# Later modulation vectors and residual additions on VectorE alone, with their loads spread differently over the stages of a decoder layer

## The chip, the cores and the metric

The kernel runs on one core of one Trainium2 chip. The metric is the device time of one execution in microseconds (us); lower is better. All arithmetic is in float32, and the large products are made from float32 numbers split into a high and a low part.

## The reference

One decoder layer: an adaLN-conditioned mixer (sparse attention and stick-breaking attention on eight heads each), then an adaLN-conditioned mixture of 32 experts. What the change touches are the six modulation vectors and the gated residual:

```
mod = jax.nn.silu(c) @ w_mod[l] + b_mod[l]                    # (1, 2048) @ (2048, 6 * 2048)
sh1, sc1, g1, sh2, sc2, g2 = split(mod, 6)
h = rms_norm(x, ln1_g[l]) * (1.0 + sc1) + sh1
x = x + g1 * hybrid_mixer(h, w_in[l], ..., w_out[l])          # 512 tokens, 2048 wide
h = rms_norm(x, ln2_g[l]) * (1.0 + sc2) + sh2
x = x + g2 * hierarchical_moe(h, router_g, router_e, w_gate[l], w_up[l], w_down[l])
```

Each expert has three matrices of 4 MB, so the 32 experts are 403 MB of weights, all of which are read.

## The kernel before

The program has two halves. In the first it makes h, the projections (stages named B0 to B5 and Q0 to Q3, each a 2048 x 512 or 512 x 512 piece of a weight), the two attentions, and the output projection (stages O0 to O5: O0 and O1 are the first two weight tiles of output columns 0 to 511 and 512 to 1023, O2 and O3 the other two, O4 and O5 all four of the third and fourth column block). In the second half it works through 16 pairs of experts.

Every engine runs its own instructions in the order in which the program writes them. All weights go through one list, `items`, which the SyncE queue loads in order into 8 KB slots of one pool of 23 (`big`); a load waits until its slot is free. A weight tile of 1 MB is used in two halves: ScalarE copies the high part into a tile `hl`, VectorE (GpSimd in Q0 to B3) subtracts it to get the low part, and TensorE makes 24 matmuls of 128x512 from it. The halves are prepared one half ahead of their use (two in B0).

The four later modulation vectors (SC2, G1, SH2, G2, in this order) are made row block by row block: 16 loads of 1 MB each (`w_m`, 128 x 2048), and for each one `acc += w * s` with a scalar for each partition (`gemv`). Before, VectorE takes the first 1280, 1536, 1280 or 768 columns of SC2, G1, SH2 and G2; for the rest ScalarE multiplies and GpSimd adds. `MODS` says how many of the 61 loads (three come earlier) go between the weight tiles of each group of stages in `SEGS`: B0 B4 Q2 Q3, then Q0 Q1 B1, then B3, B5, O0 O1, and O2 to O5. Each `gemv` stands on VectorE's queue ahead of the next half's subtraction.

At the end of an output stage `add_up` multiplies the four PSUM tiles by G1 on VectorE and adds them to x; before, GpSimd makes the addition except for the last stage (O5). Beside all this, lanes of attention work (index scores, top-k, softmax, the stick-breaking chains `st`) are stepped between the matmuls; B0 to Q3 and B5 to O0 carry the `st` chains, Q0 to B3 the index, top-k and sparse attention.

Of the kernel before, what the change touches and what calls it, by code (L numbers as in the profile page):

```python
# [15 lines left out]
AF = mybir.ActivationFunctionType  # L16
OP = mybir.AluOpType
# [21 lines left out]

ORDER = ("B0", "B4", "Q2", "Q3", "Q0", "Q1", "B1", "B3", "B5")  # L40
SEGS = ("B0 B4 Q2 Q3", "Q0 Q1 B1", "B3", "B5", "O0 O1", "O2 O3 O4 O5")
MODS = (5, 7, 4, 11, 4, 30)
RATES = (1.2, 1.4, 1.1, 1.5, 0.6, 0.95, 0.2, 0.8, 0.65)
ROOM = (3, 3, 4)
PRE = 3
FAR = ("B0",)
SHARE = 6
CUT = (1280, 1280, 1536, 768)


class Lanes:
# [26 lines left out]
def tile_hybrid_layer(ctx: ExitStack, tc, A, out, dbg=None):  # L78
# [10 lines left out]
    def slot(shape, dt=F32, name="b"):  # L89
        t = big.tile(shape, dt, name=name, tag="b")  # L90
        return t

    def bank(tag, name, dt=F32):
        t = ps.tile([P, 512], dt, name=name, tag=tag)
        return t

    V, G, T, SC, Q = nc.vector, nc.gpsimd, nc.tensor, nc.scalar, nc.sync

    def act(o, i, f=AF.Copy, **kw):
        return SC.activation(o, i, f, **kw)  # L100

    def mm(o, l, r, start, stop, skip=False):
        return T.matmul(o, l, r, start=start, stop=stop, skip_group_check=skip)  # L103
# [5 lines left out]
    def k2(shape, name, dt=F32):  # L109
        t = sm.tile(shape, dt, name=name, tag="k2", bufs=4)  # L110
        return t
# [33 lines left out]
    sil = sm.tile([P, 16], F32, name="sil")  # L145
# [23 lines left out]
    w_dc_v = w_down.rearrange("e (j p) d -> e p j d", p=P)  # L169

    SH1, SC1, G1, SH2, SC2, G2 = range(6)
    CUTS = {SC2: CUT[0], SH2: CUT[1], G1: CUT[2], G2: CUT[3]}
    BCOL = 848

    def src(it):
# [45 lines left out]
    def spread(ws, n):  # L221
        ws = [p for w in ws for p in halves(w)]
        for k, w in enumerate(ws):
            items.append(w)
            for _ in range(n * (k + 1) // len(ws) - n * k // len(ws)):
                items.append(later.pop(0))
# [4 lines left out]
    seg = [sum((work[n] for n in names.split()), []) for names in SEGS]  # L231
    for ws, n in zip(seg, MODS):
        spread(ws, n)
# [36 lines left out]
    accs, rowv = {}, {}  # L270


    def gemv(acc, w, s, cut, first):

        lo, hi = slice(0, cut), slice(cut, acc.shape[-1])
        if first:
            V.tensor_scalar(acc[:, lo], w[:, lo], s, None, op0=OP.mult)
            act(acc[:, hi], w[:, hi], AF.Identity, scale=s)
        else:
            V.scalar_tensor_tensor(acc[:, lo], w[:, lo], s, acc[:, lo], op0=OP.mult, op1=OP.add)  # L280
            act(w[:, hi], w[:, hi], AF.Identity, scale=s)
            G.tensor_tensor(acc[:, hi], acc[:, hi], w[:, hi], op=OP.add)  # L282

    def mod_chunk(v, c, q, lag):

        w = raw.pop(("m", v, c, q))
        if c is None:
            if q == 0:
                accs[v] = slot([P, D], name=f"accv{v}")
                if v in (G1, G2):  # L290
                    G.memset(accs[v], 0.0)
                    G.dma_start(accs[v][0:1], A["b_gate"][int(v == G2):int(v == G2) + 1])
            gemv(accs[v], w, sil[:, q:q + 1], CUTS[v], q == 0 and v not in (G1, G2))
            if q == 15:
                for b in range(4):
                    deferred.append([lag + b // 2, lambda b=b: mod_done(v, b, accs[v][:, 512 * b:512 * b + 512])])
            return
        o, n, r = PIECES[c]
        if q == 0:
            accs[v, c] = k2([P, n], f"acc{v}{c}") if v == SH1 and c else bank("at", f"md{v}{c}")  # L300
        acc = accs[v, c]
        for i in range(r):
            s = sil[:, r * q + i:r * q + i + 1]
            if v == SC1 or c == 0:
                k = 32 * (i % 4)
                mm(acc[k:k + 32, :n], s.to_broadcast([P, 32]), w[:, i], q == 0 and i < 4, r * q + i >= 12, True)
            else:
                gemv(acc, w[:, i], s, n * SHARE // 16, q == 0 and i == 0)

    def first_cols(c):  # L310
        o, n, _ = PIECES[c]
# [31 lines left out]
    def mod_done(v, c, acc):  # L343
        pb = bank("at", f"md{v}{c}")
        if v in (G1, G2):
            mm(pb, ones, acc, True, True)
            act(acc, pb)
            rowv[v] = accs[v]
            return
        l = acc.rearrange("p (q j) -> p j q", j=4)  # L350
        for j in range(4):
            for q in range(4):
                qs = slice(32 * q, 32 * q + 32)
                mm(pb[qs, j:j + 1], l[:, j, qs], one1, True, True)
        cs = slice(4 * c, 4 * c + 4)
        bo, dst = {SC2: (V_SC2, a2), SH2: (V_SH2, sh2)}[v]
        V.tensor_tensor(dst[:, cs], pb[:, :4], vecs[:, bo + 4 * c:bo + 4 * c + 4], op=OP.add)
        if v == SC2:
            V.scalar_tensor_tensor(dst[:, cs], dst[:, cs], 1.0, vecs[:, V_LN2 + 4 * c:V_LN2 + 4 * c + 4],
                                   op0=OP.add, op1=OP.mult)  # L360
# [591 lines left out]
    x1 = []  # L952
# [24 lines left out]
    def main_o(c, q, h, start, stop):  # L977
        wH, wL = HL.pop(("O", c, q, h))
        if start:
            mbanks["b"] = [bank("mm", f"O{c}{i}") for i in range(4)]  # L980
        if q == 0 and h == 0:
            xc = slot([P, 4, 512], name=f"x1_{c}")
            Q.dma_start(xc, x_v[:, :, 512 * c:512 * c + 512])
            x1.append(xc)
        pm = mbanks["b"]
        oH, oL = oS[q // 2, q % 2]
        for t in range(4):
            ts = slice(128 * t, 128 * t + 128)
            for jj in range(2):
                j = 2 * h + jj  # L990
                first, last = start and jj == 0, stop and jj == 1
                mm(pm[t], oH[:, j, ts], wH[:, jj], first, False)
                mm(pm[t], oH[:, j, ts], wL[:, jj], False, False)
                mm(pm[t], oL[:, j, ts], wH[:, jj], False, last)
            if (c, q, h) == (3, 3, 1):
                add_up(c, t, pm, V)
                keep(c, t)
                if t:
                    turn(c, t - 1)
                if t > 1:  # L1000
                    route(c, t - 2)
            yield
        if stop:
            if c == 3:
                turn(c, 3)
                route(c, 2)
                route(c, 3)
                V.tensor_reduce(rs, ssx, axis=AX.X, op=OP.add)
                rstd(r2, rs, D)
            while len(deferred) > (2 if c == 3 else 0):  # L1010
                later_run()
            if c < 3:
                for t in range(4):
                    add_up(c, t, pm, G)
                if q == 3:
                    keep(c)
                    lanes.add(0, resid(c))
# [1 line left out]
    r2, rs = (sm.tile([P, 4], F32, name=n) for n in ("r2", "rs"))  # L1019
    x1T = {}  # L1020

    def add_up(c, t, pm, eng):
        tmp = sm.tile([P, S], F32, name="mix", tag="tmp", bufs=3)
        V.tensor_tensor(tmp, pm[t], rowv[G1][:, 512 * c:512 * c + 512], op=OP.mult)
        eng.tensor_tensor(x1[c][:, t], x1[c][:, t], tmp, op=OP.add)

    x1d = dram.tile([S, D], F32, name="x1d")

    def keep(c, t=None):

        ts = slice(0, 4) if t is None else slice(t, t + 1)
        G.dma_start(x1d.rearrange("(t p) d -> p t d", p=P)[:, ts, 512 * c:512 * c + 512], x1[c][:, ts])

    def turn(c, t):

        pt = bank("at", "x1t")
        for j in range(4):
            T.transpose(pt[:, 128 * j:128 * j + 128], x1[c][:, t].rearrange("p (k j) -> p j k", j=4)[:, j], ident)
        x1T[t] = sm.tile([P, S], F32, name="x1T", tag="rb", bufs=2)
        jk = sm.tile([P, S], F32, name="jk", tag="tmp", bufs=3)  # L1040
        if (c, t) == (3, 3):
            act(jk, x1[c][:, t], AF.Square, accum_out=ssx[:, t, c:c + 1])
            act(x1T[t], pt)
        else:
            act(x1T[t], pt)
            act(jk, x1[c][:, t], AF.Square, accum_out=ssx[:, t, c:c + 1])

    def route(c, t):
        for j in range(4):
            mm(rt[0][:, 36 * t:36 * t + 36], x1T[t][:, 128 * j:128 * j + 128], R3[:, 4 * c + j],  # L1050
               c == 0 and t == 0 and j == 0, c == 3 and t == 3 and j == 3, True)
# [35 lines left out]
    def st(shape, name):  # L1087
# [4 lines left out]
                    op=OP.mult)  # L1092
# [38 lines left out]
    tmp = sm.tile([P, 4, 4, 8], F32, name="lsel", tag="tmp", bufs=3)  # L1131
# [140 lines left out]
    acc = x1  # L1272
# [88 lines left out]
    for n in range(NP):  # L1361
        pgu = []
        i = 24 * n
# [70 lines left out]
    with tc.If(reg > 0):  # L1434
# [13 lines left out]
        with tc.For_i(0, reg, 1):  # L1448
# [23 lines left out]
            for pk, wv in zip(pgu, (w_g_v, w_u_v)):  # L1472
                for c in range(4):
                    w = slot([P, 4, 512], name="wo")
# [5 lines left out]
            for f in range(4):  # L1480
                w = slot([P, D], name="wo")
# [74 lines left out]
```

## Time and profile before

| | |
|---|---|
| median of 3 runs | 1900.78 us (1898.29 to 1902.36) |
| the profiled execution's own time | 1895.36 us |
| its span in the profile | 1893.6 us |
| busy: TensorE, VectorE, ScalarE, GpSimd | 92%, 51%, 32%, 21% of the span |
| data moved | 585.09 MB |

The span is what the profile's times run over; the execution's own time is 1.8 us longer. The shares are means over stages with different limits, so they say little about one stage.

### The profile page before, as it was taken

The numbers are of one execution on the slowest core, as the hardware profiler recorded it, in microseconds if no ns is written. First come the engines' busy times: TensorE is split into PE (matmuls) and PEld (weight loads), VectorE is DVE, ScalarE is ACT, GpSimd is POOL, SyncE is SP. The second block draws the span as 40 slices with busy tenths as digits, with TensorE's granted clock in tenths as the row PEclk, the third lists the DMA queues.
The fourth block names the chain that finished last, engine by engine and source line by source line (L and its number), as shares of the span: only waits on it lengthen the run. The fifth ranks groups of instructions, "written<-read, shape, count | busy, mean of one in ns | idle before, by whom it ended". The sixth has DMA issues, their size and how long they took to land.

```text
span 1893.6 us, 21355 instructions
## 1 busy us (share of the span) xinstructions
PE 1740.0 (92%) x8097; PEld 976.8 (52%) x8097; DVE 973.5 (51%) x1486; ACT 601.5 (32%) x1136; POOL 396.2 (21%) x311
## 2 busy tenths in 40 slices
PE   4999999998999998899899999999999999999997
PEld 1777777765677676787334333333333333333333
DVE  6888722488855668768334334342433243333325
ACT  3645444554556543443222110111012111211010
POOL 3534311333437326656100000000000000000000
PEclk9999999999999998999999999999999999999999
DMA  9878322323226657768899999999999999999997
GB/s 349 285 263 300 123 79 94 133 90 111 90 89 224 227 178 267 267 245 354 359 418 420 419 420 418 420 419 419 419 420 419 420 419 420 419 420 419 419 413 275
DMA packets 136634, 585.09 MB, mean 309 GB/s; under 512 B 10866, under 2 KB 43802, under 8 KB 79270
## 3 DMA queue, kind: packets, MB, share of 16 engines
q1 hardware_dynamic: 132240, 569.09, 76.6%
q0 software_dynamic: 4288, 14.60, 2.1%
q8 instruction: 65, 1.06, 0.2%
q14 instruction: 41, 0.34, 0.0%
HBM read 583.64 MB, written 8.40 MB: 313 GB/s over the span
## 4 chain that ended last, share of the span: by engine, by line
DMA 39%; PE 20%; DVE 6%; issue 4%; ACT 2%; POOL 1%; SPq 0%; DVEq 0%; POOLq 0%; ACTq 0%
DMA w_u<-in_w_up 15%; DMA w_g<-in_w_gate 12%; DMA w_d<-in_w_down 12%; PE O L103 5%; PE y L103 3%; PE u L103 3%; PE g L103 2%; PE B L103 2%; DVE hl L394 1%; PE cb L103 1%; DVE accv L280 1%; DVE x L1288 1%; PE z L103 1%; PE ga L1252 1%; DMA xg<-x1d,gi 1%
## 5 line engine op out<-in xcount | busy, mean ns | idle before, releaser
L103 PE MATMUL u<-w_u,xe 128*64 128x512 f32 x1024 | 265.8, 605 | 24.4 <-DMA w_u<-in_w_up 23.7
L103 PE MATMUL g<-w_g,xe 128*64 128x512 f32 x1024 | 240.9, 596 | 18.4 <-DMA w_g<-in_w_gate 17.4
L1288 DVE TENSOR_TENSOR x<-cb,x 128x512 f32<-128x512 f32 x256 | 157.3, 682 | 186.7 <-PE cb L103 186.7
L103 PE MATMUL y<-w_d,uT 128*64 128x512 f32 x1024 | 236.9, 600 | 0.7 <-ACT uT L100 0.7
L282 POOL TENSOR_TENSOR accv<-accv,w_m_None 128x768 f32<-128x768 f32 (+2 forms) x62 | 153.0, 2468 | 210.6 <-ACT w_m_None L100 124.0
L1230 POOL DMA_INDIRECT xg<-x1d,gi x15 | 15.2, 1016 | 816.4 <-DVE t L1233 654.9
L103 PEld LDWEIGHTS u<-w_u,xe 128*64 128x64 f32 x1024 | 78.2, 138 | 201.5 <-issue 138.1
L103 PEld LDWEIGHTS g<-w_g,xe 128*64 128x64 f32 x1024 | 76.3, 137 | 170.5 <-issue 129.3
L1278 DVE SCALAR_TENSOR_TENSOR yt<-y,gs,accv 128x512 f32<-128x512 f32 x64 | 47.8, 747 | 200.5 <-PE y L103 200.5
L280 DVE SCALAR_TENSOR_TENSOR accv<-w_m_None,sil,accv 128x1280 f32<-128x1280 f32 (+2 forms) x62 | 132.6, 2138 | 6.2 <-issue 5.5
L100 ACT ACTIVATE xe<-ga,modc 128x128 f32<-128x128 f32 x254 | 94.1, 463 | 128.6 <-PE y L103 88.4
L103 PEld LDWEIGHTS y<-w_d,uT 128*64 128x64 f32 x1024 | 66.6, 136 | 116.1 <-issue 106.7
L100 ACT ACTIVATE uT<-uT 128x512 f32<-128x512 f32 x16 | 9.6, 600 | 343.4 <-PE uT L1329 343.4
L103 PE MATMUL cb<-yH,oT 128*128 128x512 f32 x256 | 107.8, 421 | 0.9 <-DVE x L1288 0.9
L100 ACT ACTIVATE yH<-yt 128x512 fp32r<-128x512 f32 x64 | 40.3, 630 | 204.5 <-DVE yt L1278 121.4
L103 PE MATMUL cb<-yL,oT 128*128 128x512 f32 x256 | 101.1, 395 | 0.0
L1280 DVE TENSOR_TENSOR yL<-yt,yH 128x512 fp32r<-128x512 f32 x64 | 44.3, 693 | 110.3 <-PE g L103 63.2
L394 DVE TENSOR_TENSOR hl<-w_O,hl 128x1024 fp32r<-128x1024 f32 x32 | 67.8, 2123 | 40.1 <-ACT hl L100 31.2
L282 POOL TENSOR_TENSOR acc<-acc,w_m 128x160 f32<-128x160 f32 x105 | 61.3, 584 | 70.1 <-ACT w_m L100 62.4
L103 PEld LDWEIGHTS cb<-yH,oT 128*128 128x128 f32 x256 | 48.0, 188 | 49.6 <-issue 38.6
L1252 PEld LDWEIGHTS ga<-cst,xg 128*128 128x128 f32 x252 | 35.2, 209 | 61.8 <-issue 41.0
L1323 DVE TENSOR_TENSOR u<-sg,u 128x512 f32<-128x512 f32 x16 | 11.0, 689 | 105.4 <-PE u L103 105.4
(435 smaller groups left out, 3171.5 us busy)
## 6 DMA issues: line engine op xcount, KB each, us to landing
w_g<-in_w_gate SPq DMA_DIRECT2D x128, 1024.0 KB, 19.9
w_u<-in_w_up SPq DMA_DIRECT2D x128, 1024.0 KB, 21.2
w_d<-in_w_down SPq DMA_DIRECT2D x128, 1024.0 KB, 19.9
w_m_None<-in_w_mod SPq DMA_DIRECT2D x64, 1024.0 KB, 5.0
w_m<-in_w_mod SPq DMA_DIRECT2D x32, 1024.0 KB, 11.0
w_B<-in_w_in SPq DMA_DIRECT2D x48, 512.0 KB, 4.7
w_O<-in_w_out SPq DMA_DIRECT2D x16, 1024.0 KB, 5.9
w_A<-in_w_in SPq DMA_DIRECT2D x8, 848.0 KB, 11.7
```

Of the source, the lines that this page charges most:

```text
L100: return SC.activation(o, i, f, **kw)
L103: return T.matmul(o, l, r, start=start, stop=stop, skip_group_check=skip)
L280: V.scalar_tensor_tensor(acc[:, lo], w[:, lo], s, acc[:, lo], op0=OP.mult, op1=OP.add)
L282: G.tensor_tensor(acc[:, hi], acc[:, hi], w[:, hi], op=OP.add)
L394: low_eng[0].tensor_tensor(t[:, 1], s, t[:, 0].bitcast(F32), op=OP.subtract)
L1230: G.indirect_dma_start(xs, None, x1d[:, :], bass.IndirectOffsetOnAxis(ap=gi[:, 0:1], axis=0), bounds_check=S - 1, oob_is_err=False)
L1252: T.transpose(pb[:, 128 * j:128 * j + 128], xs[:, 512 * c:512 * c + 512].rearrange("p (k j) -> p j k", j=4)[:, j], ident)
L1278: V.scalar_tensor_tensor(yt, y, g, rowv[G2][:, cs], op0=OP.mult, op1=OP.mult)
L1280: V.tensor_tensor(yL[:, cs], yt, yH[:, cs].bitcast(F32), op=OP.subtract)
L1288: return lambda: V.tensor_tensor(acc[q][:, t], pb, acc[q][:, t], op=OP.add)
L1323: V.tensor_tensor(u, sg, pb, op=OP.mult)
```

## The change

Each `gemv` of the four later vectors is one VectorE instruction over all 2048 columns; ScalarE and GpSimd have no part in it any more. The residual additions of all output stages go from GpSimd to VectorE. The loads are dealt out anew by `MODS`. The early vectors (`w_m` in pieces) keep their split, which is now handed in as a number.

```diff
-MODS = (5, 7, 4, 11, 4, 30)
+MODS = (20, 2, 6, 12, 4, 17)
...
-CUT = (1280, 1280, 1536, 768)
...
-    def gemv(acc, w, s, cut, first):
+    def gemv(acc, w, s, first, cut=None):
 
         lo, hi = slice(0, cut), slice(cut, acc.shape[-1])
         if first:
             V.tensor_scalar(acc[:, lo], w[:, lo], s, None, op0=OP.mult)
-            act(acc[:, hi], w[:, hi], AF.Identity, scale=s)
         else:
             V.scalar_tensor_tensor(acc[:, lo], w[:, lo], s, acc[:, lo], op0=OP.mult, op1=OP.add)
-            act(w[:, hi], w[:, hi], AF.Identity, scale=s)
-            G.tensor_tensor(acc[:, hi], acc[:, hi], w[:, hi], op=OP.add)
+        if cut:
+            act(acc[:, hi] if first else w[:, hi], w[:, hi], AF.Identity, scale=s)
+            if not first:
+                G.tensor_tensor(acc[:, hi], acc[:, hi], w[:, hi], op=OP.add)
...
-            gemv(accs[v], w, sil[:, q:q + 1], CUTS[v], q == 0 and v not in (G1, G2))
+            gemv(accs[v], w, sil[:, q:q + 1], q == 0 and v not in (G1, G2))
...
             if c < 3:
                 for t in range(4):
-                    add_up(c, t, pm, G)
+                    add_up(c, t, pm)
...
-        eng.tensor_tensor(x1[c][:, t], x1[c][:, t], tmp, op=OP.add)
+        V.tensor_tensor(x1[c][:, t], x1[c][:, t], tmp, op=OP.add)
```

On VectorE in stage O5 (the last output stage; `accv5` is G2, `hl` the low part of an output weight) these rows stand before:

```order
L394 TENSOR_TENSOR hl_6101<-w_O_3_1_5949,hl_6101 128x1024
L280 SCALAR_TENSOR_TENSOR accv5_5692<-w_m_5_None_9_6048,sil_84,accv5_5692 128x768
L280 SCALAR_TENSOR_TENSOR accv5_5692<-w_m_5_None_10_6094,sil_84,accv5_5692 128x768
L394 TENSOR_TENSOR hl_6138<-w_O_3_2_6099,hl_6138 128x1024
L280 SCALAR_TENSOR_TENSOR accv5_5692<-w_m_5_None_11_6128,sil_84,accv5_5692 128x768
L394 TENSOR_TENSOR hl_6172<-w_O_3_2_6099,hl_6172 128x1024
L280 SCALAR_TENSOR_TENSOR accv5_5692<-w_m_5_None_12_6136,sil_84,accv5_5692 128x768
L394 TENSOR_TENSOR hl_6204<-w_O_3_3_6165,hl_6204 128x1024
```

and these in the changed kernel, at the same place:

```order
L393 TENSOR_TENSOR hl_5996<-w_O_3_1_5813,hl_5996 128x1024
L277 SCALAR_TENSOR_TENSOR accv5_5205<-w_m_5_None_12_5947,sil_84,accv5_5205 128x2048
L393 TENSOR_TENSOR hl_6028<-w_O_3_2_5993,hl_6028 128x1024
L393 TENSOR_TENSOR hl_6057<-w_O_3_2_5993,hl_6057 128x1024
L277 SCALAR_TENSOR_TENSOR accv5_5205<-w_m_5_None_13_6023,sil_84,accv5_5205 128x2048
L393 TENSOR_TENSOR hl_6087<-w_O_3_3_6026,hl_6087 128x1024
```

Fewer modulation steps stand between the subtractions, each over the full width; GpSimd, which had one addition of 1280 columns for each of them, has none.

On VectorE in stage B4 (`accv4` is SC2, `st` the stick-breaking chains) these rows stand before:

```order
L394 TENSOR_TENSOR hl_2053<-w_B_4_0_1961,hl_2053 128x1024
L813 SCALAR_TENSOR_TENSOR st_2095<-z_2096,st_2095 128x384
L813 SCALAR_TENSOR_TENSOR st_2101<-z_2102,st_2101 128x384
L394 TENSOR_TENSOR hl_2147<-w_B_4_1_2018,hl_2147 128x1024
L813 SCALAR_TENSOR_TENSOR st_2095<-z_2157,st_2095 128x384
L813 SCALAR_TENSOR_TENSOR st_2101<-z_2166,st_2101 128x384
L394 TENSOR_TENSOR hl_2197<-w_B_4_1_2018,hl_2197 128x1024
```

and these in the changed kernel:

```order
L393 TENSOR_TENSOR hl_2067<-w_B_4_0_1998,hl_2067 128x1024
L812 SCALAR_TENSOR_TENSOR st_2109<-z_2110,st_2109 128x384
L812 SCALAR_TENSOR_TENSOR st_2115<-z_2116,st_2115 128x384
L277 SCALAR_TENSOR_TENSOR accv4_1662<-w_m_4_None_12_2032,sil_84,accv4_1662 128x2048
L393 TENSOR_TENSOR hl_2161<-w_B_4_1_2061,hl_2161 128x1024
L812 SCALAR_TENSOR_TENSOR st_2109<-z_2171,st_2109 128x384
L812 SCALAR_TENSOR_TENSOR st_2115<-z_2180,st_2115 128x384
L277 SCALAR_TENSOR_TENSOR accv4_1662<-w_m_4_None_13_2065,sil_84,accv4_1662 128x2048
L393 TENSOR_TENSOR hl_2217<-w_B_4_1_2061,hl_2217 128x1024
```

A modulation step of full width now stands ahead of the subtraction of every half.

## Rows read from the trace of the kernel before

**Rows 1.** The page: busy time by engine, and the chain that ended last.

```profile
PE 1740.0 (92%) x8097; PEld 976.8 (52%) x8097; DVE 973.5 (51%) x1486; ACT 601.5 (32%) x1136; POOL 396.2 (21%) x311
...
DMA 39%; PE 20%; DVE 6%; issue 4%; ACT 2%; POOL 1%; SPq 0%; DVEq 0%; POOLq 0%; ACTq 0%
```

**Rows 2.** Windows: length; busy of PE, PEld, DVE, ACT, POOL (instructions); granted clock; DMA share; GB/s.

```profile
199.00:387.00 188.00, 184.03 (x804) 137.44 (x803) 75.78 (x92) 89.32 (x148) 47.27 (x38) 1.00 0.30 101
387.00:484.00 97.00, 86.84 (x353) 58.36 (x352) 87.07 (x184) 50.67 (x109) 32.84 (x15) 0.93 0.29 98
484.00:710.00 226.00, 212.75 (x1005) 157.53 (x1004) 143.20 (x175) 122.16 (x220) 91.59 (x60) 0.98 0.47 169
710.00:897.00 187.00, 168.36 (x919) 140.29 (x919) 145.69 (x89) 75.16 (x102) 120.72 (x56) 0.94 0.76 281
897.00:956.00 59.00, 46.63 (x230) 20.99 (x231) 22.33 (x84) 13.43 (x31) 5.56 (x5) 0.94 0.92 372
956.00:1082.00 126.00, 124.71 (x574) 49.61 (x571) 43.38 (x79) 25.82 (x61) 2.20 (x2) 1.00 1.01 419
1082.00:1894.00 812.00, 752.57 (x3174) 292.81 (x3171) 288.89 (x527) 121.26 (x273) 11.99 (x12) 0.99 1.00 410
```

**Rows 3.** The chain that ended last: start, length in us, what.

```profile
820.63 12.46 PE O L103 x54
...
869.55 3.61 issue
873.16 3.72 DVE accv L280
876.88 3.89 DVE hl L394
```

**Rows 4.** VectorE's timeline while GpSimd does nothing: start, length in us, what.

```profile
302.69 1.23 DVE L394 TENSOR_TENSOR hl<-w_B,hl 128x1024 fp32r<-128x1024 f32 x1 [1.17 <-ACT hl L100]
303.84 1.55 DVE L280 SCALAR_TENSOR_TENSOR accv<-w_m_None,sil,accv 128x1280 f32<-128x1280 f32 x1
...
666.82 1.81 DVE L280 SCALAR_TENSOR_TENSOR accv<-w_m_None,sil,accv 128x1536 f32<-128x1536 f32 x1
...
839.41 1.00 DVE L280 SCALAR_TENSOR_TENSOR accv<-w_m_None,sil,accv 128x768 f32<-128x768 f32 x1
```

**Rows 5.** GpSimd's timeline in O5: one addition by itself, then eight in a row.

```profile
845.81 2.93 POOL L282 TENSOR_TENSOR accv<-accv,w_m_None 128x1280 f32<-128x1280 f32 x1 [6.65 <-ACT w_m_None L100]
849.93 29.75 POOL L282 TENSOR_TENSOR accv<-accv,w_m_None 128x1280 f32<-128x1280 f32 x8 [1.19 <-ACT w_m_None L100]
```

**Rows 6.** Windows of line 280 (VectorE's modulation steps): busy us (instructions); 575 to 647 is B5.

```profile
199.00:387.00 188.00, 13.98 (x7) 1.00 0.30 101
387.00:484.00 97.00, 10.30 (x5) 0.93 0.29 98
484.00:710.00 226.00, 36.55 (x18) 0.98 0.47 169
575.00:647.00 72.00, 19.89 (x10) 1.00 0.57 210
710.00:897.00 187.00, 68.63 (x30) 0.94 0.76 281
```

**Rows 7.** Windows of line 394 alone (subtractions): VectorE, GpSimd.

```profile
710.00:897.00 187.00, 54.27 (x23) 0.00 (x0) 0.94 0.76 281
```

**Rows 8.** Waits of TensorE in 710 to 897: total us, times, longest.

```profile
PE O L103 <- DVE hl L394: 16.0, 4, 6.2
```

**Rows 9.** The same in 575 to 647 (B5).

```profile
PE z L103 <- DVE st L813: 2.6, 3, 1.6
```

**Rows 10.** Groups by form: the residual additions on VectorE (O5).

```profile
L1025 DVE TENSOR_TENSOR x<-x,mix 128x512 f32<-128x512 f32 x4 | 2.8, 692 | 0.1
```

**Rows 11.** Waits of the SyncE queue in 199 to 387.

```profile
SPq L256 <- DVE hl L394: 48.1, 5, 18.6
```

**Rows 12.** The page's DMA issues: KB each, median us from issue to landing.

```profile
w_m_None<-in_w_mod SPq DMA_DIRECT2D x64, 1024.0 KB, 5.0
```

More of the change, by code (lines that the diff above doesn't have):

```diff
@@ L171, in tile_hybrid_layer @@
     SH1, SC1, G1, SH2, SC2, G2 = range(6)
-    CUTS = {SC2: CUT[0], SH2: CUT[1], G1: CUT[2], G2: CUT[3]}
     BCOL = 848
@@ L307, in mod_chunk @@
             else:
-                gemv(acc, w[:, i], s, n * SHARE // 16, q == 0 and i == 0)
+                gemv(acc, w[:, i], s, q == 0 and i == 0, n * SHARE // 16)
     def first_cols(c):
@@ L995, in main_o @@
             if (c, q, h) == (3, 3, 1):
-                add_up(c, t, pm, V)
+                add_up(c, t, pm)
                 keep(c, t)
@@ L1013, in main_o @@
                 for t in range(4):
-                    add_up(c, t, pm, G)
+                    add_up(c, t, pm)
                 if q == 3:
@@ L1020, in tile_hybrid_layer, with add_up @@
     x1T = {}
-    def add_up(c, t, pm, eng):
+    def add_up(c, t, pm):
         tmp = sm.tile([P, S], F32, name="mix", tag="tmp", bufs=3)
         V.tensor_tensor(tmp, pm[t], rowv[G1][:, 512 * c:512 * c + 512], op=OP.mult)
-        eng.tensor_tensor(x1[c][:, t], x1[c][:, t], tmp, op=OP.add)
+        V.tensor_tensor(x1[c][:, t], x1[c][:, t], tmp, op=OP.add)
     x1d = dram.tile([S, D], F32, name="x1d")
```

## The prediction

> **What bounds the kernel now.** I read the page first. TensorE is busy for 92% of the span and VectorE for 51%, but the chain that ended last is 39% DMA [rows 1], so there are at least two regimes. The windows separate them [rows 2]. From 956 us on, the DMA share is 1.00 or more at 410 to 419 GB/s: the expert half is bound by the weight stream, and no edit here touches it. It begins when the output projection and the routing behind it (897 to 956) are done. So a microsecond saved before 897 should move everything behind it by a microsecond, and the question is what bounds each stage before 897.
>
> In 199 to 387 (B0, B4, the Q stages) TensorE is busy for 184.0 of 188.0 us at full clock, and VectorE for 75.8: TensorE is the bound and VectorE has room. In 387 to 484 (B1) it turns round: VectorE is busy for 87.1 of 97 us, TensorE idle for 10.2, and its granted clock is 0.93. In 484 to 710 (B3, B5, O0, O1) TensorE is busy for 212.8 of 226 us. In 710 to 897 (O2 to O5) VectorE has 145.7 and GpSimd 120.7 of 187 us, while TensorE is idle for 18.6 us at a clock of 0.94 [rows 2]. Of that idle time 16.0 us are spent waiting for the subtraction `hl` on VectorE [rows 8], and the chain there alternates modulation steps, unnamed waits and subtractions on VectorE [rows 3].
>
> Why VectorE is late is seen by holding its rows alone against rows beside GpSimd. A modulation step of 768 columns takes 1.00 us alone [rows 4], but 3.72 us in the chain, where a subtraction of 1.23 us takes 3.89 [rows 3, 4]. GpSimd's addition of 1280 columns takes 2.93 us by itself, and eight in a row take 29.75, that is 3.72 each [rows 5]. Adding 1.00 to 2.93 gives 3.93, close to both: in O5 the two engines work one after the other, not side by side. The split of one modulation step over them therefore costs VectorE about as much time as the whole step would.
>
> **The change part by part.**
>
> *A step of 2048 columns on VectorE* isn't in the trace. From 768 columns at 1.00 us to 1536 at 1.81 us [rows 4] a column costs 0.81 / 768 = 1.055 ns, and 1.81 + 512 x 1.055 ns = 2.35 us. Bounds: not below the 1.81 us of 1536 columns, and not above a 768 and a 1280 step together, 1.00 + 1.55 = 2.55 us. I take 2.35, since three rows lie on that line.
>
> The Trainium skill, GPSIMD Engine Reference, section "Elementwise — side-by-side cycle accounting", gives 2293 ns for a VectorE addition of 2048 float32 columns. By that figure the 17 steps of O2 to O5 would come to 39.0 us; no run shown has that width.
>
> *O2 to O5.* 30 steps (68.6 us of VectorE [rows 6], and 30 GpSimd additions) become 17 of 2.35 us, 40.0 us. The 23 subtractions there take 54.3 us [rows 7]; alone they are 23 x 1.23 = 28.3 us, so 26.0 us go with GpSimd's load. 12 residual additions come over from GpSimd at 0.69 us [rows 10], 8.3 us. VectorE: 145.7 - 68.6 + 40.0 - 26.0 + 8.3 = 99.4 us, well below what TensorE needs. TensorE's own work bounds the gain: O2 to O5 have 24 halves of 24 matmuls, 576 at 12.46 / 54 = 0.231 us [rows 3], 133 us, and the turning of x and the router come on top. What can go is the idle 18.6 us and what the low clock costs. If the clock is either full or half (2.4 or 1.2 GHz), a mean of 0.94 means half level for 12% of 187 us, 22.4 us, and up to 11.2 us lost. The ceiling is 18.6 + 11.2 = 30 us. I take 24: the stall before the router's scaled weights and the ends of stages remain, where two multiply-and-add pairs now stand ahead of the next step on VectorE instead of two multiplications. The low end is 12, about two thirds of the idle time.
>
> *B1.* Five steps (10.3 us [rows 6]) become two, 4.7 us, and five GpSimd additions vanish; the GpSimd subtractions stay. VectorE is relieved of 5.6 us and of the waiting behind those additions. By the same reckoning the ceiling is 10.2 idle + half of 14% of 97 us (6.8) = 17 us; the floor is nothing, if the attention's own chain of ScalarE and VectorE sets the pace. I take 7.
>
> *199 to 387.* Seven steps (14.0 us [rows 6]) become 20, 47.0 us, so VectorE rises from 75.8 to some 109 of 188 us. TensorE's work covers it, as long as no subtraction and no `st` step comes late. What stands behind each new step on VectorE is the next half's subtraction and the next `st` step, and TensorE waits for both in order. The nearest row is B5, where sticks run beside ten steps [rows 6]: TensorE waited 2.6 us for `st` [rows 9], 0.26 us a step, so 13 more steps cost 3.4. Bounds: nothing, and all of 13 x 2.35 = 31 us if every step delayed TensorE in full. I take a loss of 4.
>
> *The rest.* B3 to O1 go from 18 steps [rows 6] to 22 (six, twelve and four), 36.5 to 51.7 us, and eight residual additions come over, 5.5 us; there GpSimd's additions vanish as well. VectorE goes from 143.2 to about 164 of 226 us, still behind TensorE's 212.8. The two roughly cancel; I take a gain of 1, within -3 to +5. ScalarE loses its multiplications everywhere; it is busy for under 60% of each stretch [rows 2], so that is worth nothing. The 13 loads moved from O2 to O5 cost the DMA nothing: 13.6 MB more in 188 us on top of 101 GB/s make 173 GB/s, far below 419 [rows 2].
>
> *Sum.* 24 + 7 - 4 + 1 = 28 us. The profiled execution's own time is 1895.4 us, so 1867.4; the median of the runs lies 5.4 us above that execution, which makes **1872 us** rounded down from 1872.8.
>
> One rule speaks against the change. What the rows say of it: VectorE would be worse off only where it is the bound, which is B1 alone, and there its load falls; in the two stretches where it takes work on or over, it ends at 109 of 188 and at 99 us. The Trainium skill, Perfetto Trace Analysis, section "Optimizing Scalar/DVE Operations", says that with a saturated VectorE, moving work to ScalarE or GpSimd may help, though between GpSimd and VectorE perhaps not. By its first half undoing the split would make O2 to O5 slower; by the rows of O5, where both engines are slow together, its second half holds.
>
> **The rivals.**
>
> *The weights of 199 to 387 come late (slower).* All loads share one in-order queue and 23 slots, and there the queue already waits, 48.1 us for subtractions alone [rows 11]. With 20 modulation tiles between twelve weight tiles (eight for B0 and B4, four for the Q stages), a weight load can be let go only when a modulation step has freed a slot; it then lands 5 us later [rows 12]. If each of the twelve stalls TensorE for a landing, that is 60 us: 1900.8 - 32 + 60 = 1929. It outweighs the gain from the seventh tile on (32 / 5). For it: the slots are scarce. Against it: in O2 to O5 the queue carried 1.25 modulation tiles for each half, more than the one now, and its largest wait on TensorE was for VectorE [rows 8]; and the data come at 173 of 419 GB/s.
>
> *The gain is given back, or doesn't get through (same).* Either every new step in 199 to 387 lands on TensorE in full (31 us against 32), or the expert stream was full already before 897, so that ending O5 sooner starts nothing sooner. Against the first stand 112 idle us of VectorE in those 188; against the second the DMA share of 0.76 and 0.92 ahead of 956 [rows 2]. Some 1899.
>
> *More comes back.* If VectorE's relief empties all idle time and restores the clock in both places: 30 + 17 + 3 = 50 us, 1851. For it: B1 has VectorE at 90%, and nothing else near that.
>
> **How the numbers follow.** The forecast has 0.75, "more" 0.12, "same" 0.05, "slower" 0.08. Within 0.2% (3.8 us) is about what a measurement of this kernel can't tell from no change; so faster 0.87, same 0.05, slower 0.08. The range runs from the "more" case, 1852, to 1890, where O2 to O5 give 12, B1 3 and 199 to 387 costs 4: what is slower than that has little over 0.1.
>
> **What would show it.** After the change, the steps of line 277 (the former 280) should take 2.2 to 2.5 us with hardly any spread, the subtractions in the O stages 1.23, and GpSimd should be all but idle from O1 on. O2 to O5 should last about 163 us with a clock near 1.00, B1 about 90, and 199 to 387 at most 195. The stretch from the end of O5 to the end of the span should stay at 997 us (1893.6 - 897). The forecast is wrong if subtractions wait for ScalarE copies that wait for `w_B` in 199 to 387, if TensorE's waits there name `st` for more than 10 us, or if the stretch behind O5 grows by what the stretch before it loses.

## The result, and the profile after

The changed kernel takes 1889.15 us (median of 8 runs, 1886.49 to 1895.9) against 1899.15 us of the kernel before (8 runs, 1896.8 to 1902.36) on the same chip: ratio 0.9948, 95% interval 0.9934 to 0.9961. It is faster by about 10 us, where 28 were forecast. The profiled execution has a span of 1886.4 us against 1893.6.

Two lines of the page answer to [rows 1]: busy time by engine, and the chain that ended last. One more is the group of the new steps (instructions, busy us, mean ns, idle time before them).

```profile
PE 1734.4 (92%) x8097; PEld 976.0 (52%) x8097; DVE 954.4 (51%) x1506; ACT 543.7 (29%) x1072; POOL 227.1 (12%) x229
...
DMA 42%; PE 31%; DVE 17%; issue 4%; ACT 4%; POOL 1%; SPq 0%; DVEq 0%; ACTq 0%; POOLq 0%
...
L277 DVE SCALAR_TENSOR_TENSOR accv<-w_m_None,sil,accv 128x2048 f32<-128x2048 f32 x62 | 150.5, 2427 | 8.0 <-DMA accv<-in_b_gate 6.1
```

The windows of the changed kernel answer to [rows 2], cut where its own stages begin: B0; B4; the Q stages; B1; B3 to O1; O2 to O5 (up to the last output matmul).

```profile
200.70:255.00 54.30, 50.91 (x209) 39.32 (x208) 43.77 (x43) 17.73 (x26) 1.51 (x2) 0.97 0.66 233
255.00:340.70 85.70, 74.67 (x416) 54.84 (x415) 33.45 (x32) 29.26 (x48) 13.38 (x14) 0.94 0.40 138
340.70:408.40 67.70, 67.48 (x309) 48.49 (x308) 27.57 (x42) 37.06 (x67) 20.13 (x15) 1.00 0.31 106
408.40:498.50 90.10, 81.79 (x354) 56.15 (x352) 80.88 (x179) 46.07 (x104) 21.51 (x10) 0.96 0.25 82
498.50:726.40 227.90, 211.69 (x878) 156.69 (x877) 152.54 (x175) 109.91 (x201) 59.21 (x35) 0.98 0.49 172
726.40:890.30 163.90, 158.51 (x899) 133.42 (x898) 92.27 (x87) 40.59 (x66) 8.12 (x9) 0.99 0.70 257
```

The kernel before, cut in the same way, for B4 and for O2 to O5:

```profile
251.60:319.00 67.40, 66.61 (x287) 50.01 (x286) 18.90 (x19) 33.32 (x53) 11.50 (x14) 1.00 0.23 78
709.90:894.10 184.20, 165.93 (x898) 137.95 (x899) 144.24 (x86) 72.89 (x96) 120.28 (x55) 0.94 0.76 279
```

The reader is to see two stages. O2 to O5 fell from 184.2 to 163.9 us and TensorE fills it at a clock of 0.99. B4 rose from 67.4 to 85.7 us, although VectorE is busy there for only 33.45 of the 85.7: VectorE's time isn't what B4 lacks. Of the 18.3 us, 10.2 are idle time of TensorE (11.0 against 0.8). Its busy time grew by 8.1; 2.3 of that are 128 small matmuls that turn the finished SC2 and lay in B3 before, so some 5.8 go with the clock of 0.94.

In O2 to O5 the wait for `hl` that was 16.0 us before [rows 8] is

```profile
PE O L102 <- DVE hl L393: 0.8, 1, 0.8
```

All stages, in us, from the starts of their first main matmuls in TensorE's timeline (rows that begin with o are runs described below):

| kernel | start of B0 | B0 to Q1 (B4 alone) | B1 | B3 to O1 | O2 to O5 | behind | span |
|---|---|---|---|---|---|---|---|
| before | 199.1 | 187.7 (67.4) | 96.8 | 226.3 | 184.2 | 999.5 | 1893.6 |
| after | 200.7 | 207.7 (85.7) | 90.1 | 227.9 | 163.9 | 996.1 | 1886.4 |
| o e1_old_mods | 199.8 | 185.0 (67.4) | 97.9 | 220.0 | 164.1 | 1000.2 | 1867.1 |
| o e2_mods_only | 200.7 | 216.3 (86.7) | 88.6 | 237.1 | 166.0 | 999.9 | 1908.5 |
| o e6_two_ahead | 200.1 | 198.7 (78.5) | 91.2 | 227.9 | 163.9 | 997.6 | 1879.3 |
| o e7_balanced | 199.7 | 185.2 (67.4) | 90.1 | 230.8 | 164.3 | 999.4 | 1869.5 |
| o e9_one_slot_held | 199.9 | 201.8 (84.3) | 97.4 | 218.9 | 164.8 | 999.8 | 1882.6 |

How TensorE loses its time in B4 is followed over three engines. ScalarE, 288 to 312 us (start, length, what, in brackets the idle time before it and what ended it):

```profile
288.55 0.62 ACT L99 ACTIVATE st<-st,one 128x384 f32<-128x384 f32 x1
297.46 1.06 ACT L99 ACTIVATE hl<-w_B 128x1024 fp32r<-128x1024 f32 x1 [8.29 <-PE B L102]
298.42 0.85 ACT L99 ACTIVATE st<-z 128x384 f32<-128x384 f32 x2
...
299.86 0.61 ACT L99 ACTIVATE st<-st,one 128x384 f32<-128x384 f32 x1
309.54 1.06 ACT L99 ACTIVATE hl<-w_B 128x1024 fp32r<-128x1024 f32 x1 [9.06 <-DVE accv L277]
```

VectorE there:

```profile
289.68 2.34 DVE L277 SCALAR_TENSOR_TENSOR accv<-w_m_None,sil,accv 128x2048 f32<-128x2048 f32 x1
298.55 1.22 DVE L393 TENSOR_TENSOR hl<-w_B,hl 128x1024 fp32r<-128x1024 f32 x1 [6.53 <-ACT hl L99]
300.51 0.56 DVE L812 SCALAR_TENSOR_TENSOR st<-z,st 128x384 f32<-128x384 f32 x1 [0.74 <-ACT st L99]
```

TensorE there:

```profile
301.21 0.78 PE L102 MATMUL z<-st,mone 128*128 128x256 f32 x2 [3.79 <-DVE st L812]
```

A copy into `hl` stands at the head of ScalarE's queue and waits 8.29 us for the matmuls `B` that still read an older tile: `hl` comes from the same pool of 23 slots as the loads, and the slot that the copy is to fill is still in use. (The copy reads `w_B` alone, which no matmul writes, so it can't be waiting for data.) The activations of the stick-breaking chain (`st`) behind it have to wait too, so VectorE's `st` step comes at 300.51, and the matmul at 301.21 has waited 3.79 us. The waits of ScalarE in all of B4 name what the copies wait for (total, times, longest):

```profile
ACT hl L99 <- DVE accv L277: 15.5, 3, 9.1
ACT hl L99 <- PE md L102: 10.5, 1, 10.5
...
ACT hl L99 <- PE B L102: 9.1, 2, 8.3
```

These are the users of slots: modulation tiles, SC2's vector (free only when the matmuls `md` have turned it) and older `hl` tiles. That is 35.1 us, where the `hl` copies in B4 of the kernel before waited 7.8 us. TensorE's waits in the same stretch answer to [rows 9]:

```profile
PE z L102 <- DVE st L812: 6.9, 2, 3.8
PE pob L102 <- ACT B L99: 2.2, 1, 2.2
PE B L102 <- ACT hl L99: 1.2, 1, 1.2
PE B L102 <- DVE hl L393: 0.8, 1, 0.8
```

No weight's DMA stands in this list. That the slots are the cause was only a reading of the trace at this point; the runs below test it.

### The profile page after: what moved, and what is told of

Same layout as the page of the kernel before. It is cut to its first block, busy times and chain, and to the rows that moved or that the text cites. A ratio compares the mean times of both kernels' runs of the same rounds, so it can differ in the third digit from the quotient of the medians.

```text
span 1886.4 us, 21166 instructions
## 1 busy us (share of the span) xinstructions
PE 1734.4 (92%) x8097; PEld 976.0 (52%) x8097; DVE 954.4 (51%) x1506; ACT 543.7 (29%) x1072; POOL 227.1 (12%) x229
## 4 chain that ended last, share of the span: by engine, by line
DMA 42%; PE 31%; DVE 17%; issue 4%; ACT 4%; POOL 1%; SPq 0%; DVEq 0%; ACTq 0%; POOLq 0%
DMA w_u<-in_w_up 15%; DMA w_g<-in_w_gate 13%; DMA w_d<-in_w_down 13%; PE O L102 8%; PE B L102 7%; DVE acc L277 3%; PE y L102 3%; PE Q L102 2%; PE u L102 2%; PE g L102 2%; PE z L102 2%; DVE accv L277 2%; DVE sel L731 1%; PE cb L102 1%; PE pob L102 1%
## 5 line engine op out<-in xcount | busy, mean ns | idle before, releaser
L102 PE MATMUL g<-w_g,xe 128*64 128x512 f32 x1024 | 241.3, 596 | 19.8 <-DMA w_g<-in_w_gate 19.6
L102 PEld LDWEIGHTS u<-w_u,xe 128*64 128x64 f32 x1024 | 77.8, 136 | 198.7 <-issue 135.5
L277 DVE SCALAR_TENSOR_TENSOR accv<-w_m_None,sil,accv 128x2048 f32<-128x2048 f32 x62 | 150.5, 2427 | 8.0 <-DMA accv<-in_b_gate 6.1
L99 ACT ACTIVATE hl<-w_B 128x1024 fp32r<-128x1024 f32 x48 | 50.5, 1053 | 54.5 <-DVE accv L277 30.3
L393 POOL TENSOR_TENSOR hl<-w_B,hl 128x1024 fp32r<-128x1024 f32 x17 | 48.0, 2822 | 143.8 <-ACT hl L99 113.5
```

What stands on the lines that cost most here:

```text
L393: low_eng[0].tensor_tensor(t[:, 1], s, t[:, 0].bitcast(F32), op=OP.subtract)
```

## The experiments

The expectations name theories by letters. A: the dealing of 20 loads to B0 to Q3 costs the time, above all where SC2 ends and G1 begins inside B4 (there VectorE also waits for G1's bias row). B: the gain in O2 to O5 comes from the new dealing, and the freed GpSimd does little. C: each modulation step costs by the time that it takes of VectorE. D, formed after the first four runs: the slots of the pool run out, and an `hl` copy that waits for one holds up ScalarE's queue.

**The two parts apart.** e1_old_mods is the changed kernel with the old dealing:

```diff
-MODS = (20, 2, 6, 12, 4, 17)
+MODS = (5, 7, 4, 11, 4, 30)
```

> The changed kernel with the old dealing of loads (5, 7, 4, 11, 4, 30); steps and residual additions stay on VectorE alone. Theory A (the 20 us lost from B0 to Q1 come from the loads put there, above all from the end of SC2 and the start of G1 inside B4): 199 to 387 is back at 188 us; O2 to O5 have 13 more steps of 2.4 us on VectorE, some 130 of 163 us, so they keep 20 of their 24 us; B1 keeps about 5 of 7. Some 1874 us. Rival B (the new dealing is what empties O2 to O5, the freed GpSimd does little): O2 to O5 fall back to 180 or more and the kernel to 1890 to 1900 us.

Measured: 1867.34 us, ratio 0.9832 (0.9815 to 0.9848). It is the fastest of all kernels here, about 22 us ahead of the change as a whole. e2_mods_only is the kernel before with the new dealing:

```diff
-MODS = (5, 7, 4, 11, 4, 30)
+MODS = (20, 2, 6, 12, 4, 17)
```

> The kernel before with the new dealing of loads (20, 2, 6, 12, 4, 17) alone; steps stay split over VectorE, ScalarE and GpSimd. Theory A: 199 to 387 loses the same 20 us or more, since loads and change-over are there, with 1.55 us steps on VectorE; O2 to O5 gain about half (17 GpSimd additions instead of 30), some 12. About 1907 us, slower than before. Rival C (the loss in B4 is VectorE's time, 2.35 us for each full step): the loss falls to about two thirds, 13 us, and the kernel stays near 1900.

Measured: 1909.58 us, ratio 1.0053 (1.0037 to 1.007). So VectorE alone gains 31 us and the dealing by itself loses 10; the two together gain 10, not 21, since both mend the same stall. That is seen in the windows of O2 to O5. In e1, with 30 full-width steps on VectorE:

```profile
249.60:317.00 67.40, 66.61 (x286) 50.01 (x286) 18.78 (x19) 31.63 (x51) 6.42 (x12) 1.00 0.23 78
702.80:866.90 164.10, 159.51 (x899) 134.08 (x899) 123.11 (x102) 40.84 (x66) 8.18 (x9) 0.98 0.85 320
```

and in e2, with 17 steps that are still split:

```profile
742.70:908.65 165.95, 160.97 (x898) 135.28 (x899) 109.77 (x73) 61.34 (x83) 87.70 (x42) 0.97 0.65 240
```

Either part alone brings O2 to O5 from 184.2 to 164 or 166 us; with both it is 163.9. So B is half right: the dealing relieves O2 to O5 too, but it isn't needed for that. B4 is at 67.4 us in e1, as before, and at 86.7 in e2: its loss belongs to the dealing.

**A dose between.** e3_fewer_early is the changed kernel with

```diff
+MODS = (12, 3, 8, 12, 6, 20)
```

> The changed kernel with (12, 3, 8, 12, 6, 20): 12 loads in B0 to Q3 instead of 20, so that SC2 ends in Q1 and G1 begins in B1, not in B4. Theory A: B4 is back at 68 us or less, 199 to 387 loses at most 4 us, O2 to O5 stay at 165; about 1875 us. Rival C (VectorE's time for each step): the loss shrinks only in proportion, 5 steps more than before instead of 13, 8 us left, B4 near 74; about 1879 us.

Measured: ratio 0.988 (0.9861 to 0.9899). Of its five executions the profiled one took 9487 us; it is left out, so there are no stage times. The other four lie between 1874.1 and 1879.8 us, with a median of 1876.3. That is between the two forecasts, 1875 and 1879, and doesn't tell A and C apart.

**G1's bias.** e4_no_gate_bias takes away the cleared start and the bias row of G1 and G2, so that VectorE's first step waits for no DMA:

```diff
-                if v in (G1, G2):
-                    G.memset(accs[v], 0.0)
-                    G.dma_start(accs[v][0:1], A["b_gate"][int(v == G2):int(v == G2) + 1])
-            gemv(accs[v], w, sil[:, q:q + 1], q == 0 and v not in (G1, G2))
+            gemv(accs[v], w, sil[:, q:q + 1], q == 0)
```

> The changed kernel without the bias of the two gate vectors: their first step writes the accumulator, so that no memset and no bias DMA stand ahead of it (the output lacks b_mod for g1 and g2). Theory A: the hold of VectorE at 301 to 307 us goes, with the two late st steps behind it, and B0 to Q1 get back 8 to 12 of the 20 us; about 1879 us. Rival C: nothing to speak of, 1 to 2 us.

Measured: 1891.05 us, ratio 0.9956 (0.9939 to 0.9972); B0 to Q1 take 211.0 us. The wait of 6.1 us is gone and nothing is gained: this part of A falls.

**Short steps.** e5_short_steps cuts the steps of SC2 and the first seven of G1 to 256 columns; the loads and their slots stay.

```diff
-        lo, hi = slice(0, cut), slice(cut, acc.shape[-1])
+        lo, hi = slice(0, 256 if short and not first else cut), slice(cut, acc.shape[-1])
...
+                 short=v == SC2 or (v == G1 and q < 7))
```

> The changed kernel with all loads, but the 20 steps in B0 to Q3 (SC2 and the first of G1) made over 256 of the 2048 columns, so that VectorE spends some 9 us on them instead of 47 (the rest of these two vectors is left out, so the routing and the time behind the projection are not compared). Theory D (the 23 slots run out in B4: ScalarE's copy of a half waits at the head of its queue for a slot, and the stick steps behind it come late): B0 to Q1 still take 203 us or more. Rival C (VectorE's time for the steps): they fall to 190 us.

Measured, in a single execution: 1892.31 us. The steps of B4 come to 3.82 us in the window of their line alone (18.76 in the changed kernel), yet B4 takes 88.0 us:

```profile
251.60:339.60 88.00, 3.82 (x8) 0.88 0.38 133
```

The `hl` copies wait 37.1 us there (21.6 + 13.8 + 1.7). B0 to Q1 take 206.6 us, 1.1 less than with full steps (207.7): B0 gives back 3.4 us, B4 is 2.3 longer. C falls for B4: VectorE's time for the steps is not the price there.

**One load less ahead.** e6_two_ahead lets the queue run two items ahead instead of three from B0 to Q3:

```diff
     lanes.add(1, make_tb())
+    AHEAD = 2
...
+    AHEAD = 3
     low_eng[0] = G
```

> The changed kernel with loads running two items ahead instead of three from B0 to Q3, so that one slot fewer is held by tiles that lie waiting. Theory D: ScalarE's waits for slots in B4 shrink, B0 to Q1 get back 8 us or more of the 20, unless a load now lands late; about 1880 us. Rival C: no gain, 1889 us or more.

Measured: 1884.01 us, ratio 0.992 (0.9905 to 0.9935). B4 falls from 85.7 to 78.5 us, and B0 to Q1 get back 9.0. Asking for fewer loads ahead makes the stage faster, which speaks for slots and against late loads.

**The early part as before, B1 relieved.** e7_balanced:

```diff
+MODS = (5, 2, 8, 12, 4, 30)
```

> The changed kernel with (5, 2, 8, 12, 4, 30): as few loads in B0 to Q3 as before the change, as few in Q0 to B1 as after it. Theory D: B0 to Q1 stay at 185 us as with the old dealing, B1 gets back its 6 us, O2 to O5 stay at 166; some 1861 us. Rival: B1 gains only when GpSimd and VectorE are relieved together with what comes before it, and the time stays at 1867.

Measured: 1871.29 us, ratio 0.9861 (0.9843 to 0.9879): 10 us above what D was taken to say, and no better than e1. B1 came to 90.1 us as hoped, but B3, with 8 steps and the end of SC2 in it, takes 102.9 instead of 91.7 in e1. ScalarE's waits in B3 of e7 again name slots:

```profile
ACT hl L99 <- DVE accv L277: 10.1, 3, 7.8
```

**The additions.** e8_gpsimd_adds puts the residual additions of O0 to O4 back on GpSimd:

```diff
-                    add_up(c, t, pm)
+                    add_up(c, t, pm, G)
...
-        V.tensor_tensor(x1[c][:, t], x1[c][:, t], tmp, op=OP.add)
+        eng.tensor_tensor(x1[c][:, t], x1[c][:, t], tmp, op=OP.add)
```

> The changed kernel with the residual additions of O0 to O4 on GpSimd again (the loads and the steps as in the change). If VectorE has room in O2 to O5, as 99 of 163 us say, nothing moves by more than 3 us. Rival: the additions keep VectorE from freeing the PSUM tiles at a stage's end (TensorE waited 3.4 us for that between O0 and O1), and it gains 3 to 5 us.

Measured: 1886.2 us, ratio 0.9927 (0.9909 to 0.9945), which overlaps with the changed kernel's interval. With the old dealing the same edit, e12_old_mods_gpsimd_adds, was run last:

> This is the old dealing (5, 7, 4, 11, 4, 30) with the modulation steps on VectorE alone, and the residual additions of all but the last output stage back on GpSimd: the part of the change that is left when both other parts are taken back. If the additions are hidden on VectorE (TensorE is the bound of the output stages), it stands where the same kernel with the additions on VectorE stood, ratio 0.983 (1865 to 1870). If the 2.5 to 3 us by which the changed kernel with its additions on GpSimd was faster are real, it stands at 0.9815 (about 1864). The forecast's reading, that GpSimd's work is paid by VectorE anyway, allows a loss of at most 2 us.

Measured: 1874.0 us, ratio 0.9872 (0.9856 to 0.9889), which is some 4 parts in 1000 above e1 and outside of both expectations. Its O2 to O5 take 166.3 us against 164.1 in e1. The additions are worth a few us with one dealing and nothing that can be told with the other; why they differ stays open.

**A slot taken away.** e9_one_slot_held turns the test round. It is the fast kernel e1, with one slot held by an unused tile during B4; no load and no step is moved.

```diff
+    held = [slot([P, D], name="held") for _ in range(1)]
+    for t in held:
+        G.memset(t[:, 0:2], 0.0)
     steps("B4", RATES[0])
+    for t in held:
+        act(t[:, 0:1], t[:, 1:2])
```

> This is the fast kernel of the old dealing (VectorE alone, 5 modulation loads from B0 to Q3, 1867.3 us) with one slot of the pool taken by an unused tile from the start to the end of B4: two words are written on GpSimd when B4 starts, and ScalarE reads one of them behind its last copy of B4. No load is added, no modulation step moved. Theory D (slots): B4 grows from 67.4 us by about what one slot was worth when the loads ran two instead of three ahead (7 us), and ScalarE's waits in B4 name copies into hl for more than the 8 us they had; time about 1874, not under 1870. The rival (steps or loads of the modulation vectors cost by themselves, whatever the slots): B4 stays at 67 to 68 us and the time at 1866 to 1869.

Measured: 1885.11 us, ratio 0.9925 (0.9904 to 0.9946). B4 goes from 67.4 to 84.3 us, by its own window to 84.4:

```profile
249.60:334.00 84.40, 72.25 (x288) 52.47 (x286) 19.63 (x19) 31.66 (x52) 5.95 (x12) 0.94 0.22 75
```

and ScalarE's waits in it are

```profile
ACT hl L99 <- PE B L102: 30.0, 5, 10.1
...
ACT hl L99 <- PE pob L102: 3.4, 1, 3.4
ACT hl L99 <- DVE accv L277: 3.1, 1, 3.1
```

36.5 us of waiting `hl` copies, where e1 has 3.1 + 2.5 + 2.2 = 7.8:

```profile
ACT hl L99 <- PE B L102: 3.1, 3, 1.1
ACT hl L99 <- PE pob L102: 2.5, 1, 2.5
ACT hl L99 <- DVE accv L277: 2.2, 1, 2.2
```

One missing slot, with the old dealing and VectorE busy for 19.6 of 84.4 us, brings almost the whole loss of the changed kernel's B4 (16.9 of 18.3 us), the clock of 0.94 included. This is D shown directly; the size was more than twice what was expected of one slot.

**Fewer chains open.** e10_two_chains lets two chains of the first four be open instead of three:

```diff
-ROOM = (3, 3, 4)
+ROOM = (2, 3, 4)
```

> This is the changed kernel with two stick-breaking chains open at a time instead of three while the first four are begun, so one slot fewer is held by their tiles in B4; loads and modulation steps stay. Theory D: B4 falls from 85.6 us to about 78, as it did with one load less ahead (78.5), the wait of ScalarE's hl copies falls, and the time is about 1882, if the chains that start later don't cost it again in B1 to B5. The rival (the steps themselves): B4 stays at 84 to 87 us and the time at 1888 to 1892, or goes up with the later chains.

Measured: 1881.93 us, ratio 0.9911 (0.9888 to 0.9934). That the time is the expected one is luck: B4 is back at 67.3 us, better than expected, but the Q stages lose most of that again (below). Nor is the reason in B4 the expected one. The `hl` copies in it still wait 30.7 us, against 35.1 in the changed kernel:

```profile
ACT hl L99 <- PE B L102: 24.0, 4, 9.8
ACT hl L99 <- DVE accv L277: 2.9, 1, 2.9
ACT hl L99 <- PE pob L102: 2.5, 1, 2.5
ACT hl L99 <- DVE hl L393: 1.3, 1, 1.3
```

So slots stay short in B4. What is gone are the chain's activations behind the long waits: from 283.4 to 311 us ScalarE's timeline has copies alone, and no wait for `st` is left among TensorE's in B4 (0 in e1 and e10, 4.2 us in e6, 6.9 in the changed kernel, 8.0 in e5 and e9; B4 takes 67 us in the first two, 78.5 in e6, 84 to 88 in the others). In these runs a waiting copy costs time where a step that TensorE needs stands behind it. The chains that aren't done by then run in the Q stages, which take 81.8 us instead of 67.7. There TensorE waits for them:

```profile
PE z L102 <- DVE st L812: 6.5, 2, 4.7
```

So B0 to Q1 keep 203.3 of 207.7 us: the loss was moved more than mended.

**The turn put later.** e11_turn_late deals so that SC2 ends with B3 and G1 begins in B5:

```diff
+MODS = (5, 4, 4, 14, 4, 30)
```

> This is the changed kernel with 5, 4, 4, 14, 4, 30 loads, so that SC2 ends with the last step of B3 and G1 begins in B5. From the fast kernel of the old dealing (1867.3 us; B1 97.9, B3 91.7, B5 69.1): B1 has three steps fewer and should take 92 to 94 us, by the way from 97.9 at seven to 90.1 at two; B3 stays at 91 to 93; B5 has 14 steps instead of 11 and should take 69 to 72. Theory D with the slots enough in all three: 1863 (1859 to 1867). The rival, that turning SC2 into its row and beginning G1 costs some 11 us in whichever stage it falls (it lay in B4 in the changed kernel and in B3 in the run with 5, 2, 8): B5 takes 80 and the time is 1872 to 1876.

Measured: 1877.36 us, ratio 0.9883 (0.9862 to 0.9903): near the rival's figure, a little above it. B1 takes 94.3 us and B3 88.8, but B5 84.0 instead of 69.1 in e1. Waits of ScalarE in B5:

```profile
ACT hl L99 <- DVE accv L277: 8.4, 1, 8.4
```

Where the end of SC2 and the start of G1 meet a stage with many steps, that stage is longer: B4 by 18.3 us in the changed kernel, B3 by 11.2 in e7 (against e1), B5 by 14.9 in e11. In e1 they fall into B3 with its four steps, and B3 takes 91.7 us against 91.8 before. Two vectors hold a slot each for a while then. That this overlap takes the deciding slot agrees with the waits for `md` and `accv`, but no run has parted the turn from the number of steps.

## Why the prediction was right in its direction and wrong in its size

By the same cuts the spans of the two profiled executions differ by 1.6 + 20.0 - 6.7 + 1.6 - 20.3 - 3.4 = -7.2 us (table above, left to right). That the median of 1889.15 us lies just inside the stated range is luck: the range's slow end, 1890, was put together from a small gain in O2 to O5 and B1 and a loss of 4, and what was measured is 20.3 and 6.7 of gain there and a loss of 20.0. The forecast's terms one by one:

**Steps of 2048 columns, 2.35 us**: right, 2.34 to 2.35 where GpSimd is quiet; the mean of all 62 is 2.43. The Trainium skill's figure for 2048 columns of an addition (GPSIMD Engine Reference, "Elementwise — side-by-side cycle accounting", 2293 ns) is 2% lower.

**O2 to O5, a gain of 24**: nearly right, 20.3 up to the last output matmul. (The stretch behind it is 3.4 us shorter as well, but it varies between 996.0 and 1001.6 us over the runs, so this can't be put down to VectorE.) Of the 16.0 us of waits for `hl` [rows 8], 0.8 are left, and the 23 subtractions fell from 54.27 to 28.00 us, by the 26 that were forecast. That the split was slow there was the right cause, shown by e1, which leaves all 30 steps in place: they take 70.41 us (2.35 each) and the subtractions 28.05. No run parts ScalarE's share of the split from GpSimd's; that it is GpSimd rests on rows 3 to 5. Two of these were read a little too cleanly: beside the addition "by itself" a subtraction on VectorE took 3.17 us (846.66 to 849.83), and the step of 1280 columns at 303.84 ran its last 0.4 us beside a GpSimd addition. The Trainium skill's remark that moving work between these two might not help (Perfetto Trace Analysis, "Optimizing Scalar/DVE Operations") is borne out. The measurement goes further: taking the split back, ScalarE's part and the residual additions with it, gained 31 us. What the forecast didn't see is that fewer steps without this would have mended it as well (e2, 166.0), so that the 13 moved loads bought nothing here.

**B1, a gain of 7**: right in size, 6.7. But its share from GpSimd's relief is nothing: e1, with five unsplit steps, stays at 97.9 us against 96.8. It is the three steps fewer (e2: 88.6).

**B3 to O1, a gain of 1**: a loss of 1.6, within its bounds. e1 shows a gain of 6.3 there, and the dealing gives back 7.9.

**Behind O5, everything passed on**: right, 996.1 us against 999.5; no run shows more than 1001.6.

**199 to 387, a loss of 4: this step failed.** It measured 20.0, 18.3 of it in B4, and 1.6 were lost ahead of it. The bounds held it (nothing to 31), but the value was taken from B5's waits for `st` by step [rows 9], 0.26 us for each of 13 more steps, as if the price were VectorE's time. "TensorE's work covers it, as long as no subtraction and no `st` step comes late" named the right victims, and e5 shows that VectorE was not what made them late in B4. What the runs put in its place: `hl` tiles and loads share the slots, an `hl` copy whose slot is still in use stands in ScalarE's queue (35.1 us instead of 7.8), and the `st` activations queue up behind it (e9 brings this about with one slot held; e10, with no `st` behind the copies, loses nothing in B4). The forecast did read in [rows 11] that the slots were scarce, but it asked only who waits for a load. So the rival of late weights had the right resource and the wrong victim: no weight was late for TensorE, and the price was 20 us, not 60. (The 20 loads lie between ten weight tiles, not twelve: Q0 and Q1 belong to the next group of `SEGS`.) Of the signs that were to show the forecast wrong, copies that wait did come, but for slots and not for `w_B`; TensorE's waits for `st`, 7.1 us from B0 to Q1, stayed below the 10 that were named, so by that sign alone the loss would have been missed.

The best version is e1, with steps and additions on VectorE alone and the loads dealt as before: 1867.34 us.

## What to carry to other kernels

Where one pool serves both loads and the tiles that engines fill, a load dealt earlier can take a slot from a copy, and the waiting copy holds up whatever stands behind it in its engine's queue, as it did in B4: before moving loads, read the waits of that engine for its slots and what stands behind them, not only the free time of the engine that will use the loads. Idle time of VectorE (112 us in that stretch) says nothing on slots. And where a change has two parts that mend the same stall, price each as if the other were made already.

## What was unexpected

One slot of 23, held for one stage, made that stage 16.9 us longer than its 67.4, with no load and no step added. The clock took its share: with TensorE's waits in pieces of at most 4.2 us (on `st`), the granted clock of B4 was 0.94 in e9 (between the levels of 1.2 and 2.4 GHz), and the same matmuls took some 5.6 us more in e9 (72.25 against 66.61).

A residual addition of 128x512 takes VectorE 0.69 us every time; on GpSimd in e12 it varies (min, median, max in ns, first and last start, forms):

```profile
L1024 POOL TENSOR_TENSOR x<-x,mix x20: 1283/1298/3329, 680.2 to 816.8; 128x512 f32<-128x512 f32 x20
L1024 DVE TENSOR_TENSOR x<-x,mix x4: 691/691/695, 863.1 to 869.6; 128x512 f32<-128x512 f32 x4
```

So at least half of them ran at about 1.3 us and the longest took 3.33.
